# Norm weights on the transposed tokens, one operation for both directions of a recurrence, weight copies on ScalarE, later gates

## The chip, the cores and the metric

The kernel runs on one core of one Trainium2 chip. The metric is the device time of the whole kernel in microseconds (us); a profiled execution also gives a span, from the first to the last instruction. In what follows PE is TensorE (PEld its weight loads), ACT is ScalarE, DVE is VectorE, POOL is GpSimd and SP is SyncE. All times are counted from the start of the span.

## The reference

A first block (attention, a pooling mixer and a mixture of 32 experts, 256 tokens of width 1024) is followed by a second block of two layers. The change touches only the second block:

```
for layer in range(2):
    h = rms_norm_2(x, attn_norm_w[layer])
    a_q, a_i, a_zf, a_zb, a_g, b_u, c_q, c_k, c_v = split(h @ w_in[layer])
    o_a = hgrn2_mixer(a_q, a_i, a_zf, a_zb, a_g, lb_all[layer])
    o_b = fourier_mixer(b_u)
    o_c = dilated_attention_mixer(c_q, c_k, c_v, positions)
    x = x + concatenate([o_a, o_b, o_c]) @ w_out[layer]
    h = rms_norm_2(x, mlp_norm_w[layer])
    x = x + square(relu(h @ w_up[layer])) @ w_down[layer]
return rms_norm_2(x, final_norm_w)
```

`rms_norm_2(x, w)` is x times the reciprocal root of its mean square, times the weight w of each column. `hgrn2_mixer` is a gated recurrence over the 256 tokens in both directions (f = lb + (1 - lb) sigmoid(z), k = 1 - f); `dilated_attention_mixer` rotates queries and keys and takes a softmax over masked scores.

## The kernel before

Every large product is done in three matmuls on a number split in two: the high parts with each other (hi x hi), and each low part with the other's high part. ACT makes the high part of a weight (tile `wh`) by a rounding copy, DVE the low part (`wl`, the weight minus `wh`); both are tiles of 128x1024, four buffers of each, filled from f32 tiles that SP's queue loads. Where a norm weight belongs to the product, `split` gets it as `g` and does each half of a tile by itself: on ACT a copy with a scale per partition, on DVE a scalar_tensor_tensor, 128x512 each (L202 and L203). Without `g` it is one operation of 128x1024 on each engine (L206 and L207). The reciprocal root of a token's norm, `rc`, is made on POOL (L278 to L281 and L1241) from sums of squares made on ACT (L270), and is applied to the product's output.

The tokens stand transposed, as `hT`. `into_hT(t, n)` turns 128 tokens and 512 columns on PE (four transposes into one bank `tp`, L294), copies the high part on ACT (L303) and makes the low part on DVE (L304). There are four such seams of four calls: into mixer 0, MLP 0, mixer 1 and MLP 1.

A mixer does six projections `proj(c0)` of 512 columns: 512 (gates z), 0 (q and v), 1536 (queries), 2048 (keys), 2560 (values cv) and 1024 (g and u), each 48 matmuls of 128x512 into banks `b` (L230 to L232). Between groups of them `bg()` runs one step of each generator that is open:

- `hgrn`, the recurrence. Gates z are transposed (`pz`), then there are eight levels, each with a product `qt` on DVE (L1509), a product `kt` on POOL (L1513; at level 0 a copy on ACT, L1511), small matmuls `hsm` whose results `sl` are masked on DVE (L1490) and summed on POOL, and updates of the running products `hES` (L1545) and `hIP` (L1546) on DVE. Each of the four is done for the forward and the backward direction apart, 128x256 elements each.
- `evac_rot`, the rotation: `rx` and `rt` on DVE, one sum on POOL and one on DVE (L1605 to L1607), then eight transposes `prot` on PE (L1617) and copies on ACT.
- `attention`: scores `sc` (L1643), s on DVE (L1648), maximum, exponentials on ACT, scaling on POOL, transposes `pt`, copies `pT` (L1672; the first of two on DVE, the second on ACT) and products `po` (L1680).

Then follow w_out (`wo`, 96 matmuls) and the MLP, eight times `up` (96 matmuls of 128x256, L240 to L242) and `down` (48 of 128x512, `dn`). Each engine works strictly in the order in which its instructions are queued; a scheduler sets that order when the kernel is built, so a change of the code also moves instructions that it doesn't name.

## Time and profile before

| | us |
|---|---|
| median of 3 runs | 1308.5 (1306.8 to 1309.25) |
| profiled execution | 1306.97 |
| its span | 1305.2 |
| PE busy in the span | 1253.0 (96%) |
| DVE busy | 680.5 (52%) |
| ACT busy | 510.7 (39%) |
| POOL busy | 200.7 (15%) |

The mean granted clock of PE is 0.989 of full speed. The second block begins at about 664 us; mixer 0 lies at 664 to 808, MLP 0 at 808 to 984, mixer 1 at 984 to 1119 and MLP 1 at 1119 to 1296. "Busy" of PE counts matmuls that overlap in its pipeline, so one row of 0.39 us can be followed by the next after 0.23 us: the pitch, from start to start, is what a matmul costs. DVE and ACT overlap by some 0.08 us in the same way.

### The profile page before, as it was taken

The page shows a single profiled execution, that of the slowest core. Times are in us where ns is not written, and L with a number is a line of the kernel's source. Part 1 is how long each engine was busy: PE and PEld are TensorE (multiplying, and loading weights), DVE is VectorE, ACT ScalarE, POOL GpSimd, SP SyncE. Part 2 cuts the span into 40 slices and gives each one's busy share as a digit, 9 for nine tenths or more (in the row PEclk, how much of TensorE's full clock was granted, in tenths as well). Part 3 has the DMA queues.
Part 4 walks back from the last instruction along what each step waited for, and adds up shares of the span by engine and source line. Part 5 has one row for each costly group of instructions (what it writes and reads, how often), then busy time and mean ns, then how long its engine had stood idle before and what let it go on. Part 6 is the DMA issues. An engine that isn't in the chain of part 4 may idle for free. (4 is left out here: it accounts for less than half of the span.)

```text
span 1305.2 us, 19758 instructions
## 1 busy us (share of the span) xinstructions
PE 1253.0 (96%) x7985; PEld 875.2 (67%) x7985; DVE 680.5 (52%) x1164; ACT 510.7 (39%) x919; POOL 200.7 (15%) x270
## 2 busy tenths in 40 slices
PE   6999988999999999899999999999999999999997
PEld 3889976344443443333357678998988767989896
DVE  3698797122122221212157965655557994765654
ACT  2456433111110111101056465555556555655544
POOL 0011030000000000000024541211113461211211
PEclk9999998999999999999999999999999999999999
DMA  9998797999999999999975342655554423555550
GB/s 326 372 340 276 266 381 266 409 416 429 426 429 427 426 427 427 426 428 421 419 305 187 114 130 90 223 181 186 193 193 158 161 82 126 188 177 193 193 162 33
DMA packets 102597, 359.37 MB, mean 275 GB/s; under 512 B 8772, under 2 KB 17856, under 8 KB 87656
## 3 DMA queue, kind: packets, MB, share of 16 engines
q1 hardware_dynamic: 101832, 357.00, 72.1%
q8 instruction: 63, 1.03, 0.3%
q0 software_dynamic: 480, 1.07, 0.2%
q14 instruction: 30, 0.25, 0.1%
q10 hardware_dynamic: 192, 0.02, 0.0%
HBM read 357.00 MB, written 1.06 MB: 274 GB/s over the span
## 5 line engine op out<-in xcount | busy, mean ns | idle before, releaser
L207 DVE TENSOR_TENSOR wl<-w,wh 128x1024 fp32r<-128x1024 f32 x128 | 156.5, 1227 | 100.9 <-ACT wh L206 100.9
L206 ACT CAST wh<-w 128x1024 fp32r<-128x1024 f32 x128 | 134.1, 1050 | 144.4 <-PE up L241 65.8
L202 ACT ACTIVATE wh<-w,vcols 128x512 fp32r<-128x512 f32 x176 | 121.2, 718 | 78.9 <-PE dn L231 34.7
L203 DVE SCALAR_TENSOR_TENSOR wl<-w,vcols,wh 128x512 fp32r<-128x512 f32 x176 | 131.1, 778 | 36.5 <-ACT wh L202 34.4
L241 PE MATMUL up<-hT,wh 128*128 128x256 f32 x512 | 142.4, 278 | 0.0
L242 PE MATMUL up<-hT,wl 128*128 128x256 f32 x512 | 142.4, 279 | 0.0
L240 PE MATMUL up<-hT,wh 128*128 128x256 f32 x512 | 142.4, 278 | 0.0
L1015 PE MATMUL pu<-w,xT 128*64 128x512 f32 x512 | 121.5, 608 | 5.4 <-DMA w<-in_w_expert_up_dram 5.4
L1015 PE MATMUL pg<-w,xT 128*64 128x512 f32 x512 | 119.5, 604 | 0.0
L1101 ACT CAST yh<-y 128x512 fp32r<-128x512 f32 x32 | 19.8, 618 | 253.6 <-DVE y L1100 187.9
L1015 PE MATMUL py<-w,actT 128*64 128x512 f32 x480 | 108.0, 593 | 1.4 <-DMA w<-in_w_expert_down_dram 1.4
L231 PE MATMUL dn<-wh,actl 128*128 128x512 f32 x256 | 101.3, 396 | 0.0
L230 PE MATMUL dn<-wh,acth 128*128 128x512 f32 x256 | 101.2, 395 | 0.0
L232 PE MATMUL dn<-wl,acth 128*128 128x512 f32 x256 | 101.2, 396 | 0.0
L241 PEld LDWEIGHTS up<-hT,wh 128*128 128x128 f32 x512 | 96.9, 189 | 0.6
L240 PEld LDWEIGHTS up<-hT,wh 128*128 128x128 f32 x512 | 96.2, 188 | 0.6
L242 PEld LDWEIGHTS up<-hT,wl 128*128 128x128 f32 x512 | 96.0, 188 | 0.5 <-DVE wl L203 0.5
L1803 POOL TENSOR_TENSOR relu<-relu 128x256 f32<-128x256 f32 x64 | 53.6, 838 | 265.9 <-ACT relu L1802 265.9
L230 PE MATMUL b<-wh,hT 128*128 128x512 f32 x224 | 92.0, 412 | 2.4 <-ACT wh L202 1.9
L232 PE MATMUL b<-wl,hT 128*128 128x512 f32 x224 | 89.4, 403 | 2.3 <-DVE wl L207 1.5
L1100 DVE SCALAR_TENSOR_TENSOR y<-py,ws,gate 128x512 f32<-128x512 f32 x30 | 22.5, 751 | 128.7 <-PE py L1015 127.2
L1015 PEld LDWEIGHTS pu<-w,xT 128*64 128x64 f32 x512 | 38.0, 139 | 76.9 <-issue 67.1
(411 smaller groups left out, 2273.3 us busy)
## 6 DMA issues: line engine op xcount, KB each, us to landing
w<-in_w_expert_up_dram SPq DMA_DIRECT2D x26, 2048.0 KB, 25.7
w<-in_w_expert_down_dram SPq DMA_DIRECT2D x26, 2048.0 KB, 27.2
w<-in_w_expert_gate_dram SPq DMA_DIRECT2D x24, 2048.0 KB, 25.4
w<-in_w_in_dram SPq DMA_DIRECT2D x40, 1024.0 KB, 6.5
w<-in_w_up_dram SPq DMA_DIRECT2D x32, 1024.0 KB, 5.4
w<-in_w_down_dram SPq DMA_DIRECT2D x32, 1024.0 KB, 5.0
w<-in_w_ada_dram SPq DMA_DIRECT2D x24, 1024.0 KB, 9.8
w<-in_w_expert_gate_dram SPq DMA_DIRECT2D x16, 1024.0 KB, 10.3
```

Source lines behind the costliest of these rows:

```text
L202: self.nc.scalar.activation(hi[:, c], v[:, c], AF.Copy, scale=g[:, i:i + 1])
L203: self.nc.vector.scalar_tensor_tensor(lo[:, c], v[:, c], g[:, i:i + 1], hi[:, c].bitcast(F32), op0=ALU.mult, op1=ALU.subtract)
L206: self.last_hi = self.nc.scalar.copy(hi, v).ins
L207: self.last_lo = self.nc.vector.tensor_tensor(lo, v, hi, op=ALU.subtract).ins
L230: nc.tensor.matmul(ps, hT.tok(0, k, t), wh, start=first, stop=False)
L231: nc.tensor.matmul(ps, hT.tok(1, k, t), wh, start=False, stop=False)
L232: nc.tensor.matmul(ps, hT.tok(0, k, t), wl, start=False, stop=last)
L240: nc.tensor.matmul(o, hi[:, c], hT.mov(0, k), start=first and m % 2 == 0, stop=False, skip_group_check=True)
L241: nc.tensor.matmul(o, hi[:, c], hT.mov(1, k), start=False, stop=False, skip_group_check=True)
L242: nc.tensor.matmul(o, lo[:, c], hT.mov(0, k), start=False, stop=last and m % 2 == 1, skip_group_check=True)
L1015: queue["last"] = f(*args, **kw).ins
L1803: nc.gpsimd.tensor_tensor(r, r, r, op=ALU.mult)
```

## The change

Four things change, all in the second block.

1. `split` has no `g` any more: every weight tile is one operation of 128x1024 on ACT and one on DVE. The norm weight is applied in `into_hT` instead, where it is one number per partition: for each of four blocks of 128 columns a copy with a scale on ACT and a scalar_tensor_tensor on DVE, both 128x128.
2. In the recurrence `qt`, `kt`, `hES` and `hIP` are one operation each for both directions (128x512 elements), by an access pattern `runs_of` that steps from one direction's runs to the other's.
3. All copies `pT` are made by ACT.
4. In layer 0 the gates z are not read out right after their projection but at the third step of the next one, and not before the last `wh` issued until then.

```diff
+def runs_of(src, off, step, b, h, wide=True):
+    return bass.AP(tensor=src.tensor, offset=src.offset + off, ap=[list(src.ap[0]), [step, 2], [2 * h, b], [1 if wide else 0, h]])
...
-    def split(self, v, g=None):
+    def split(self, v):
         hi = self.sp.tile([128, 1024], F32R, name="wh", tag="wh")
         lo = self.sp.tile([128, 1024], F32R, name="wl", tag="wl")
-        if g is not None:
-            for i in range(2):
-                c = slice(512 * i, 512 * i + 512)
-                self.nc.scalar.activation(hi[:, c], v[:, c], AF.Copy, scale=g[:, i:i + 1])
-                self.nc.vector.scalar_tensor_tensor(lo[:, c], v[:, c], g[:, i:i + 1], hi[:, c].bitcast(F32),
-                                                    op0=ALU.mult, op1=ALU.subtract)
-            return hi, lo
         self.last_hi = self.nc.scalar.copy(hi, v).ins
         self.last_lo = self.nc.vector.tensor_tensor(lo, v, hi, op=ALU.subtract).ins
         return hi, lo
...
-    def into_hT(self, t, n):
+    def into_hT(self, g, t, n):
         src = self.transposed(self.x[:, t, n * 512:n * 512 + 512])
-        self.split_into(self.hT.t[0][n][:, t], self.hT.t[1][n][:, t], src)
+        for b in range(4):
+            hi, lo = (self.hT.t[i][n][:, t, b] for i in range(2))
+            c = g[:, 4 * n + b:4 * n + b + 1]
+            self.nc.scalar.activation(hi, src[:, b], AF.Copy, scale=c)
+            self.nc.vector.scalar_tensor_tensor(lo, src[:, b], c, hi.bitcast(F32), op0=ALU.mult, op1=ALU.subtract)
...
-                    def half(x, w, h=h):
-                        return x.rearrange("p n (b w h) -> p (n b) w h", w=2, h=h)[:, :, w]
-                    for d in range(2):
-                        nc.vector.tensor_tensor(half(qt, 1 - d), half(qd, 1 - d), half(IP[:, d], 1 - d), op=ALU.mult)
-                        if lv == 0:
-                            nc.scalar.copy(half(kt, d), half(kk[:, d], d))
-                        else:
-                            nc.gpsimd.tensor_tensor(half(kt, d), half(kk[:, d], d), half(ES[:, d], d), op=ALU.mult)
+                    nb = S // h
+                    def given(x, h=h, nb=nb):
+                        return runs_of(x, 0, (0 if tuple(x.shape[1:]) == (2, S) else 2 * S) + h, nb, h)
+                    def taken(x, h=h, nb=nb):
+                        return runs_of(x, h, (0 if tuple(x.shape[1:]) == (2, S) else 2 * S) - h, nb, h)
+                    nc.vector.tensor_tensor(taken(qt), taken(qd), taken(IP), op=ALU.mult)
+                    if lv == 0:
+                        nc.scalar.copy(given(kt), given(kk))
+                    else:
+                        nc.gpsimd.tensor_tensor(given(kt), given(kk), given(ES), op=ALU.mult)
...
-                        for d in range(2):
-                            edge = (lambda x: x[:, :, h - 1:h]) if d == 0 else (lambda x: x[:, :, 0:1])
-                            full = [128, 2 * S // (2 * h), h]
-                            ip, es = IP[:, d], ES[:, d]
-                            nc.vector.tensor_tensor(half(es, d), half(es, d), edge(half(ip, 1 - d)).to_broadcast(full), op=ALU.mult)
-                            nc.vector.tensor_tensor(half(ip, 1 - d), half(ip, 1 - d), edge(half(ip, d)).to_broadcast(full), op=ALU.mult)
+                        nc.vector.tensor_tensor(given(ES), given(ES), runs_of(IP, 2 * h - 1, 2 * S - 2 * h + 1, nb, h, False), op=ALU.mult)
+                        nc.vector.tensor_tensor(taken(IP), taken(IP), runs_of(IP, h - 1, 2 * S + 1, nb, h, False), op=ALU.mult)
...
-                        (nc.scalar.copy if j else nc.vector.tensor_copy)(pT[:, j], pt)
+                        nc.scalar.copy(pT[:, j], pt)
...
-            bgs, tail = [], []
+            bgs, tail, held = [], [], []
             def bg():
+                if held:
+                    held.append(0)
+                    if len(held) == 4:
+                        with self.tc.issue_after(self.last_hi):
+                            evac_z(512, held[0])
+                        held.clear()
...
-                self.tok_part(ps, hT, win, 0, c0, True, False, bg, g=gw[:, 0:4])
+                self.tok_part(ps, hT, win, 0, c0, True, False, bg)
                 for f in late:
                     f()
-                self.tok_part(ps, hT, win, 4, c0, False, True, bg, g=gw[:, 4:8])
+                self.tok_part(ps, hT, win, 4, c0, False, True, bg)
                 e(c0, ps)
-            proj(512, evac_z, late)
+            proj(512, (lambda c0, ps: held.append(ps)) if not layer else evac_z, late)
...
-                    late.append(partial(self.into_hT, t, n))
+                    late.append(partial(self.into_hT, gw, t, n))
...
-                        todo.append(partial(self.into_hT, t, n))
+                        todo.append(partial(self.into_hT, self.norm_cols("attn_norm_w_2", 1), t, n))
```

How the built program moves is seen at three places. The first is ACT's queue around the gates of layer 0, with `mT,ss<-xnew` the sums of squares and `wh` the weights' high parts. Before:

```order
L202 ACTIVATE wh<-w,g_748 128x512
L270 ACTIVATE mT_4637,ss<-xnew 128x512
L202 ACTIVATE wh<-w,g_748 128x512
L1433 ACT_TABLE_LOAD
L1433 ACTIVATE z<-b,rc 128x512
L270 ACTIVATE mT_4637,ss<-xnew 128x512
L202 ACTIVATE wh<-w,g_748 128x512
L1433 ACTIVATE z<-b,rc 128x512
L202 ACTIVATE wh<-w,g_748 128x512 x10
```

and after:

```order
L205 CAST wh<-w 128x1024
L301 ACTIVATE hT_79<-tp,g_748 128x128
L268 ACTIVATE mT_4637,ss<-xnew 128x512
L205 CAST wh<-w 128x1024
L301 ACTIVATE hT_79<-tp,g_748 128x128
L268 ACTIVATE mT_4637,ss<-xnew 128x512
L205 CAST wh<-w 128x1024 x2
L268 ACTIVATE mT_4637,ss<-xnew 128x512
L1436 ACT_TABLE_LOAD
L1436 ACTIVATE z<-b,rc 128x512 x2
L205 CAST wh<-w 128x1024 x4
```

Both z now stand behind the last sum of squares and behind four whole `wh`; before, a sum of squares and a `wh` stood behind the first z and all later `wh` behind the second.

The second place is DVE's queue ahead of the rotation of the keys (the rows `rx<-b,cosr` and `rt<-b,sinr` at the end). Before:

```order
L203 SCALAR_TENSOR_TENSOR wl<-w,g_748,wh 128x512
L1509 TENSOR_TENSOR qt<-hq,hIP 128x32x8 x2
L203 SCALAR_TENSOR_TENSOR wl<-w,g_748,wh 128x512 x2
L1545 TENSOR_TENSOR hES<-hES,hIP 128x32x8 x2
L1546 TENSOR_TENSOR hIP<-hIP 128x32x8 x2
L203 SCALAR_TENSOR_TENSOR wl<-w,g_748,wh 128x512 x2
L1490 TENSOR_TENSOR sl<-hsm,kmix 128x128
L203 SCALAR_TENSOR_TENSOR wl<-w,g_748,wh 128x512
L1490 TENSOR_TENSOR sl<-hsm,kmix 128x128
L1509 TENSOR_TENSOR qt<-hq,hIP 128x16x16 x2
L203 SCALAR_TENSOR_TENSOR wl<-w,g_748,wh 128x512
L1605 TENSOR_TENSOR rx<-b,cosr 128x512
```

and after:

```order
L1517 TENSOR_TENSOR qt<-hq,hIP 128x2x32x8
L206 TENSOR_TENSOR wl<-w,wh 128x1024
L1549 TENSOR_TENSOR hES<-hES,hIP 128x2x32x8
L206 TENSOR_TENSOR wl<-w,wh 128x1024
L1550 TENSOR_TENSOR hIP<-hIP 128x2x32x8
L1493 TENSOR_TENSOR sl<-hsm,kmix 128x128
L206 TENSOR_TENSOR wl<-w,wh 128x1024
L1493 TENSOR_TENSOR sl<-hsm,kmix 128x128
L1517 TENSOR_TENSOR qt<-hq,hIP 128x2x16x16
L1549 TENSOR_TENSOR hES<-hES,hIP 128x2x16x16
L1609 TENSOR_TENSOR rx<-b,cosr 128x512
```

The seven half `wl` have become three whole ones (the fourth stands just ahead of this piece), the pairs of `qt`, `hES` and `hIP` one row each, and the last `hES`, of which one half stood behind `rx`, now stands ahead of it.

The third place is ACT's queue at the seam from mixer 0 into MLP 0 (`junk,ss` are sums of squares, `hT<-tp` the transposed tokens). Before:

```order
L206 CAST wh<-w 128x1024
L202 ACTIVATE wh<-w,vcols 128x512 x3
L270 ACTIVATE junk,ss<-xnew 128x512 x2
L303 CAST hT_78<-tp 128x512 x2
L202 ACTIVATE wh<-w,vcols 128x512 x4
```

and after:

```order
L205 CAST wh<-w 128x1024 x3
L268 ACTIVATE junk,ss<-xnew 128x512 x2
L301 ACTIVATE hT_78<-tp,vcols 128x128 x4
L205 CAST wh<-w 128x1024
L301 ACTIVATE hT_78<-tp,vcols 128x128 x3
L205 CAST wh<-w 128x1024
L301 ACTIVATE hT_78<-tp,vcols 128x128
```

The two copies of 128x512 have become eight pieces of 128x128, with two whole `wh` between them.

## Rows read from the trace of the kernel before

**Rows 1.** Windows: stretch, busy us (and instructions) of each engine, PE clock, DMA.
```profile
808.00:984.00 176.00, 176.00 (x1151) 158.94 (x1149) 102.54 (x133) 98.05 (x168) 30.87 (x40) 1.00 0.57 189
```

**Rows 2.** List of waits of PE, 664 to 1305: total us, times, longest.
```profile
PE prot L1617 <- POOL rx L1607: 5.8, 2, 2.9
...
PE po L1680 <- DVE pT L1672: 2.0, 2, 1.0
...
PE b L230 <- ACT wh L202: 1.9, 2, 1.7
...
PE b L230 <- ACT hT L303: 0.5, 1, 0.5
```

**Rows 3.** Timeline of PE, POOL and ACT at the gates: start, us, [idle before <-releaser].
```profile
689.49 0.39 PE L231 MATMUL b<-wh,hT 128*128 128x512 f32 x1
...
689.72 0.40 PE L232 MATMUL b<-wl,hT 128*128 128x512 f32 x1
...
692.97 0.19 POOL L1241 TENSOR_TENSOR rc<-rs 128x1 f32<-128x1 f32 x1
...
693.20 0.69 ACT L1433 ACTIVATE z<-b,rc 128x512 f32<-128x512 f32 x1 [2.95 <-POOL rc L1241]
...
694.54 0.50 PE L230 MATMUL b<-wh,hT 128*128 128x512 f32 x1 [1.72 <-ACT wh L202]
...
699.32 0.93 PE L1446 MATMUL pz<-ident,z 128*128 128x128 f32 x7
```

**Rows 4.** Timeline of DVE and PE at the rotation, layer 0.
```profile
717.65 0.68 DVE L1605 TENSOR_TENSOR rx<-b,cosr 128x512 f32<-128x512 f32 x1
...
727.10 0.76 DVE L1545 TENSOR_TENSOR hES<-hES,hIP 128x256 f32<-128x256 f32 x2
...
728.44 1.41 DVE L203 SCALAR_TENSOR_TENSOR wl<-w,g,wh 128x512 fp32r<-128x512 f32 x2
...
732.37 0.40 PE L232 MATMUL b<-wl,hT 128*128 128x512 f32 x1
...
732.99 0.68 DVE L1605 TENSOR_TENSOR rx<-b,cosr 128x512 f32<-128x512 f32 x1
...
735.66 0.44 PE L1617 MATMUL prot<-ident,rx 128*128 128x128 f32 x2 [2.90 <-POOL rx L1607]
...
740.41 0.50 PE L230 MATMUL b<-wh,hT 128*128 128x512 f32 x1
```

**Rows 5.** Groups by form, 664 to 808: busy us, mean ns, then idle.
```profile
L207 DVE TENSOR_TENSOR wl<-w,wh 128x1024 fp32r<-128x1024 f32 x8 | 9.6, 1224 | 2.1 <-ACT wh L206 2.1
...
L1490 DVE TENSOR_TENSOR sl<-hsm,kmix 128x128 f32<-128x128 f32 x10 | 2.7, 284 | 0.6 <-PE hsm L1483 0.6
...
L1703 ACT COPY fw<-f 128x127 f32<-128x127 f32 x2 | 0.5, 264 | 0.2 <-DVE fw L1702 0.2
```

**Rows 6.** Groups by form on DVE between the rotations, 717.8 to 733.
```profile
L203 DVE SCALAR_TENSOR_TENSOR wl<-w,g,wh 128x512 fp32r<-128x512 f32 x8 | 6.7, 855 | 0.0
...
L1509 DVE TENSOR_TENSOR qt<-hq,hIP 128x256 f32<-128x256 f32 x4 | 2.1, 570 | 0.0
...
L1546 DVE TENSOR_TENSOR hIP<-hIP 128x256 f32<-128x256 f32 x4 | 2.1, 548 | 0.0
...
L1545 DVE TENSOR_TENSOR hES<-hES,hIP 128x256 f32<-128x256 f32 x4 | 1.8, 462 | 0.0
```

**Rows 7.** Timeline of ACT and DVE at the copies of attention weights.
```profile
764.26 0.56 ACT L1672 COPY pT<-pt 128x512 f32<-128x512 f32 x1
...
764.73 1.04 ACT L206 CAST wh<-w 128x1024 fp32r<-128x1024 f32 x1
...
766.06 0.68 DVE L1672 COPY pT<-pt 128x512 f32<-128x512 f32 x1
```

**Rows 8.** Timeline of ACT and DVE at the seam into MLP 0.
```profile
803.64 1.05 ACT L303 CAST hT<-tp 128x512 fp32r<-128x512 f32 x2
...
804.82 1.28 DVE L304 TENSOR_TENSOR hT<-tp,hT 128x512 fp32r<-128x512 f32 x2
```

## What I predict

> **What bounds the kernel now.** I read the windows by stage first, then the list of TensorE's (PE's) waits, then the timelines around the longest of them, then durations by form. The windows tell where nothing can be won: in the MLP stage PE is busy all 176.00 us at clock 1.00, with DVE and ACT at 58% and 56% [rows 1]. So the ACT and DVE work that the weights lose there, more than half of it by count, is worth nothing. What counts is PE's waits in the two mixers, and the list gives nearly all of them [rows 2]: 5.8 us in two waits for the rotated keys (prot on rx), 2.0 in two for the attention weights (po on pT), 1.9 in two for weights (b on wh), 0.5 for the transposed tokens (b on hT). A wait costs more than its idle time where the clock falls behind it. I therefore take each loss as elapsed time less the matmuls in it at full pitch, 0.229 us from start to start (689.49 to 689.72, [rows 3]).
>
> - First gates, layer 0: after the matmul of 689.72 the next is due at 689.95; pz starts at 699.32. In these 9.37 us the timeline has 18 matmuls (the seventh is that of 694.54), 18 x 0.229 = 4.1. Loss 5.25 us.
> - Rotated keys: last b at 732.37, b again at 740.41 [rows 4]. From 732.60 that is 7.8 us; the 8 prot, 64 hsm and 8 sc between need 2.5 by the pitches that the timeline has for such matmuls at full clock. Loss 5.3, of which 2.9 idle; the same in layer 1, by the equal second wait of [rows 2].
> - Attention weights: 1.0 per layer.
>
> Together 5.25 + 2 x 5.3 + 2 x 1.0 + 0.5 = 18.4 us. Removing waits can win no more.
>
> **The change part by part.**
>
> *Later gates (layer 0).* PE waits at 694.54 for a wh that ACT makes only behind the second z, and that z waits until POOL ends rc at 693.16 [rows 3]. Rc is itself late, since the last sum of squares stood behind the first z. The order after puts all sums of squares and four whole wh ahead of both z. Without z ahead of it I work rc forward to about 692.1 and the end of z to 692.9. PE meanwhile runs the next projection and needs z only at pz, which without the stall is due at 699.32 - 5.1 = 694.2. Margin 1.3 us, so the loss goes almost wholly: **-5.1**. If the sums of squares come later than that (they share ACT with 16 pieces of hT), 1.3 us is free and beyond it pz waits one for one: bound -4.0.
>
> *Recurrence and weights ahead of the rotated keys.* This is the large term. DVE works without a gap, and its rx for the keys begins at 732.99, though the last matmul of their projection had run by 730.05 (twelve matmuls of the next projection fill PE until 732.60). DVE is 2.9 us behind. Between the two rx groups (717.65 and 732.99, [rows 4]) the order before has 8 half wl and 4 half qt, hIP and hES each; after, 4 whole wl and 2 whole of each other. Two half wl with POOL idle beside them take 1.41 (728.44), two half hES 0.76 (727.10); 0.08 of each lies under what follows. A whole wl lasts 1.22 [rows 5], 1.15 without that 0.08, so 0.18 less than the pair. A whole recurrence operation is not in the trace; I price it by the nearest row, rx at 128x512, 0.68 or 0.60 without the 0.08, so 0.07 less than the pair. That gives 4 x 0.18 + 6 x 0.07 = 1.1 us. But the halves in this stretch are stretched: eight wl take 6.7 us where four pairs of 1.41 make 5.6, twelve of the recurrence 6.0 where six of 0.76 make 4.6 [rows 6]. Upper bound of the relief, if the whole operations escape that: 1.1 + 1.1 + 1.4 = 3.6. Lower bound: 0.7, if POOL delays whole ones a little more than halves. Ahead of the first rx group stand one whole wl less (1.15) and one hES more (0.6), of use only as far as that group's own projection is done. I take 2.0 us in layer 0 and 2.7 in layer 1, out of the 2.9. The idle then falls to 0.9 and 0.2. The idle of 1.0 at po was not followed by slow matmuls, that of 1.72 at 694.54 was; so the 2.4 us that the loss has beyond its idle go too, half of them in layer 0 (1.2) and two thirds in layer 1 (1.6). Layer 0: -3.2. Layer 1: -4.3. Together **-7.5**, bounds -1.5 and -10.
>
> A page of the Trainium skill speaks against this term. "SBUF — State Buffer", section "SBUF: two separate sides", states that a DVE operation with two SBUF inputs and a GpSimd operation that reads SBUF take one port pair in turn, and that the loser blocks for the whole instruction. By that rule POOL's kt delay DVE as much in one piece as in two, and the sum would keep the lower bound. The trace agrees in part: DVE's rows do stretch beside POOL, but to 0.86 on average from 0.71 (half of the pair), not by a whole POOL instruction.
>
> *Attention weights on ACT.* Now ACT copies at 764.26, makes a wh and copies again, while DVE's second copy ends at 766.66 without the overlap; po then starts after 1.0 us of idle [rows 7]. After, ACT has two copies, a wh and two copies behind the fourth group of exponentials: 764.26 + 2 x 0.47 + 0.95 + 2 x 0.47 = 767.1. That alone is +0.45. The scores move too: in the order after, from the first sl behind prot DVE has sl, wl, sl, qt, wl (0.2 + 1.15 + 0.2 + 0.6 + 1.15 = 3.3) and then the scores' s, which lags the resumed b by up to 1.85 us where now it starts with it. With the rx wait gone PE comes to po earlier relative to this chain. So po waits longer, by 0.45 to 1.85; I take **+1.4** per layer. That makes a wait of 2.4, longer than the 1.72 that slow matmuls followed, for which I add 0.5 per layer. Both layers: +3.8.
>
> *Norm weight on the tokens.* Each seam has 16 pieces of 128x128 on each of ACT and DVE in place of 4 operations of 128x512. ACT's nearest row is the 128x127 copy, 0.26 us, DVE's the 128x128 sl, 0.28 [rows 5]. In the built order a hi piece waits for the lo piece before it, and whole wh and wl stand between pieces. At the two seams into the MLPs PE now has the first up matmul directly behind the first tp; before, a wo stood there that no list shows waiting. That up needs two hi pieces, behind both sums of squares and a wh that is 0.3 longer: 0.3 + 0.26 + 0.1 = about +0.65 each. The rest of hT hides behind twenty wo matmuls (4.6 us). The seam into mixer 1 waits 0.5 for hT already [rows 2]; +0.15. The seam into mixer 0 I count at 0: the longer hT and the shorter weights cancel in what ACT and DVE have to do before pz. Sum **+1.4**; without the cover, see the second rival.
>
> Sum: -5.1 - 7.5 + 3.8 + 1.4 = -7.4. The profiled execution took 1306.97 us, so 1299.6; the median of the runs shown is 1.5 above it, hence **1301** against 1308.5.
>
> **Rivals.**
>
> *DVE's relief does not reach rx.* Kt becomes one operation as long as two and holds up a whole wl where it held up a half, so rx comes hardly earlier. Then it is z against po and the seams: -5.1 - 1.5 + 2.3 (po at the mean of its bounds, no slow clock) + 1.4 = -2.9, about 1305.5. For it: the stretching in [rows 6]. Against: the pairs that POOL leaves alone shorten in any case. It is where the skill's rule leads. Chance 0.17.
>
> *Slower: the pieces go back and forth.* In a seam hi and lo alternate between ACT and DVE, with a whole wl between lo pieces: 0.3 + 0.3 + 1.15 a step, three steps after the first piece, 5.2 us, against 2.3 for both tiles now [rows 8]. Where PE has run out of other matmuls by then, each of the four seams costs 2.9: +11.6 in place of the +1.4, so -7.4 + 10.2 = +2.8, about 1311. It decides once a seam costs 2.2 us on average. Against: the 4.6 us of other matmuls behind each first half. Chance 0.07. The skill has the reason for the order of such pieces ("PSUM — Partial Sum Buffer", "PSUM bank collisions raise a hardware error"): no two engines may be in one bank's quadrant at once. No row here shows one.
>
> *More than expected.* Rx starts at its projection's end in both layers, and the scores come early enough with it for po: -5.1 - 9.5 + 0.9 + 0.7 = -13, 1295.5. Chance 0.10.
>
> **How the numbers follow.** The forecast has 0.66, spread over -4 to -11. I call 0.2%, 2.6 us, what can be told from no change. Faster: 0.61 of the forecast, the 0.10, and half of the first rival: 0.79. Slower: 0.07. Same: the rest, 0.14. The range 1296 to 1306.5 takes in the first rival and reaches to the third, and leaves out the slower one.
>
> **What would show it.** Right: both z behind one another with no wait for wh between 690 and 695, and clock 1.00 there; prot idle under 1 us, and rx of the keys within 1 us of its projection's end; po idle over 2 us; the first up waiting 0.6 for hT. Wrong: prot still idle near 2.9, with whole hES or hIP at twice a half's duration or more; waits for hT of 2 us at the seams; slow matmuls behind po or prot.

## The result, and the profile after

The changed kernel is slower. Its median over seven runs is 1317.39 us (1315.93 to 1324.35) against 1309.25 us for seven runs of the kernel before on the same chip; the ratio is 1.008, with an interval of 1.0061 to 1.0100. The profiled execution took 1321.54 us (span 1319.8). DVE's busy time fell from 680.5 to 665.5 us and ACT's from 510.7 to 491.7, and the kernel became longer all the same. The two profiled executions lie on either side of their medians (1306.97 against 1309.25, 1321.54 against 1317.39), so they differ by 14.6 us where the medians differ by 8.1: what follows takes that one pair of executions apart.

Ahead of the second block's first transposes (`tp`), where nothing was changed, executions differ by several us (tp comes between 668.5 and 675.6). So I compare intervals from tp to the end: 633.8 us in the profile of before, 646.6 in that of after, 12.8 more. The table comes from the starts of PE's rows: before in us, every other column the difference to it. "prot" is the first transpose of rotated queries, then of rotated keys; "sc" the first scores, then the second group; "MLP 0" runs from the first `tp` of that seam to the first of the next.

```
interval      before  after     e1     e2     e3     e4     e5     e6     e7     e8
tp to pz        27.9  -4.08  -0.25  -4.11  -0.27  -5.13  -4.11  -5.13  -4.08  -2.28
pz to prot      23.3  +1.13  +0.00  +0.96  +0.09  +1.28  +0.96  +1.38  +0.93  +1.09
prot to prot    13.1  +2.32  +1.30  +1.23  +0.04  +1.92  +1.23  +3.31  +0.97  +2.33
prot to sc       3.0  +0.96  +1.38  +0.30  +0.12  +0.23  +0.29  +1.38  +0.23  +0.97
sc to sc         4.8  +1.59  -0.22  +0.25  +1.30  +0.22  +0.55  +0.22  +0.84  -0.17
sc to po        21.8  +1.53  +0.03  +0.44  -0.02  +0.00  +1.47  +0.00  +0.96  +2.00
po to wo        14.1  -0.67  -0.33  +0.46  +0.46  +0.01  +1.28  +1.01  +1.30  -0.66
MLP 0          180.4  +3.06  +0.00  +3.05  +0.06  +0.03  +2.24  +0.03  +2.24  +0.50
tp to pz, 1     21.1  +1.16  +0.01  +1.16  +0.01  -0.01  +1.18  -0.01  +1.18  +0.59
prot to prot    13.1  +1.01  +1.29  -0.36  -0.01  +0.01  -0.34  +1.29  -0.19  +1.00
prot to sc       2.7  +1.03  +1.34  +0.39  -0.44  -0.23  +0.58  +1.41  +0.41  +1.24
sc to sc         5.0  +0.73  +0.41  +0.96  +0.63  +1.81  +0.52  +0.01  +0.93  -0.64
sc to po        21.8  +1.53  -0.01  +0.36  -0.01  +0.03  +1.48  +0.03  +0.97  +3.75
po to wo        14.1  -0.68  -0.33  +0.45  +0.45  -0.60  +2.60  +0.99  +1.27  -0.67
tp to end      192.3  +2.25  +0.02  +2.17  -0.04  +0.06  +3.10  -0.02  +3.05  +0.50
all            633.8 +12.84  +4.64  +7.71  +2.36  -0.39 +12.97  +5.84 +10.95  +9.48
```

The gates were won (-4.1). Everything else that was to be won or to cost little went the wrong way: the keys +4.9 and +2.8 (three rows from prot to the second sc), the seams +3.1, +1.2 and +2.3, the attention +0.9 in each layer (sc to po less what po to wo gives back).

The list of PE's waits after (664 to 1322; total us, times, longest), to be held against [rows 2]:

```profile
PE prot L1621 <- POOL rx L1611: 8.0, 2, 4.1
PE pt L1675 <- DVE s L1652: 2.6, 2, 1.3
PE up L240 <- DVE wl L206: 2.3, 2, 1.1
...
PE up L238 <- ACT hT L301: 1.8, 2, 0.9
PE b L230 <- DVE wl L206: 1.2, 3, 0.5
PE prot L1621 <- DVE rx L1611: 0.8, 1, 0.8
PE b L228 <- ACT hT L301: 0.6, 1, 0.6
```

The waits for wh (1.9) and for pT (2.0) are gone. The wait for the rotated keys, which was to shrink, grew from 5.8 to 8.0, and three waits are new: pt, and two in the first `up`.

At the gates, the timeline of PE, POOL and ACT after, against [rows 3]:

```profile
690.60 0.19 POOL L1243 TENSOR_TENSOR rc<-rs 128x1 f32<-128x1 f32 x1
691.29 0.69 ACT L1436 ACTIVATE z<-b,rc 128x512 f32<-128x512 f32 x1
694.59 0.50 PE L230 MATMUL b<-wl,hT 128*128 128x512 f32 x1 [0.18 <-DVE wl L206]
...
696.25 0.69 ACT L1436 ACTIVATE z<-b,rc 128x512 f32<-128x512 f32 x1 [4.28 <-POOL rc L1243]
...
697.00 1.03 PE L1449 MATMUL pz<-ident,z 128*128 128x128 f32 x8
```

No wait for wh is left and the granted clock is 1.00 from 690 to 700. The second z now ends 0.06 us before pz: it waits for its own rc, so the margin of 1.3 is used up, near the bound of -4.0.

At the rotated keys of layer 0, the timeline of DVE, POOL and PE, against [rows 4]:

```profile
731.34 0.75 DVE L1517 TENSOR_TENSOR qt<-hq,hIP 128x512 f32<-128x512 f32 x1
731.50 1.73 POOL L1521 TENSOR_TENSOR kt<-hk,hES 128x512 f32<-128x512 f32 x1
...
732.29 0.40 PE L230 MATMUL b<-wl,hT 128*128 128x512 f32 x1
733.27 0.93 DVE L1549 TENSOR_TENSOR hES<-hES,hIP 128x512 f32<-128x512 f32 x1 [1.18 <-POOL kt L1521]
734.12 0.68 DVE L1609 TENSOR_TENSOR rx<-b,cosr 128x512 f32<-128x512 f32 x1
...
736.79 0.69 PE L1621 MATMUL prot<-ident,rx 128*128 128x128 f32 x2 [4.11 <-POOL rx L1611]
...
743.31 0.63 PE L230 MATMUL b<-wl,hT 128*128 128x512 f32 x1
743.74 0.63 PE L228 MATMUL b<-wh,hT 128*128 128x512 f32 x1
```

`hES` is updated in place, and `kt` reads the old `hES`. In one piece, the update stands still until POOL has finished the whole kt, and rx stands behind it in DVE's queue. DVE, which had no gap here before, idles 1.18 us ahead of this hES, and 3.5 in three such waits up to here. PE waits 4.11 instead of 2.90, and the matmuls that follow run for a while at a pitch of 0.43 (743.31 to 743.74).

The longer wait is not all rx's doing. Counted from tp, rx starts at 60.95 us, where before it started at 61.58: it is 0.6 earlier. PE is through with its matmuls at 59.51 in place of 61.35, 1.8 earlier, because the wait at the gates is gone. With the recurrence as before and the rest of the change (e5 below) rx starts at 59.65 in layer 0, and at 61.11 in place of 62.47 in layer 1 (from that layer's tp). So the joined recurrence delays rx by 1.3 and 1.4 us; the rest of the longer wait in layer 0 is the gates' gain, met again as a wait.

Groups by form, DVE and POOL, 664 to 820 (busy, mean ns, then idle ahead of them):

```profile
L206 DVE TENSOR_TENSOR wl<-w,wh 128x1024 fp32r<-128x1024 f32 x36 | 45.6, 1275 | 13.7 <-ACT wh L205 13.7
L1517 DVE TENSOR_TENSOR qt<-hq,hIP 128x512 f32<-128x512 f32 x8 | 7.0, 872 | 0.0
L1549 DVE TENSOR_TENSOR hES<-hES,hIP 128x512 f32<-128x512 f32 x7 | 6.2, 879 | 5.8 <-POOL kt L1521 5.8
L1550 DVE TENSOR_TENSOR hIP<-hIP 128x512 f32<-128x512 f32 x7 | 6.1, 878 | 0.1
...
L302 DVE SCALAR_TENSOR_TENSOR hT<-tp,vcols,hT 128x128 fp32r<-128x128 f32 x12 | 3.8, 344 | 2.2 <-ACT hT L301 2.2
...
L1521 POOL TENSOR_TENSOR kt<-hk,hES 128x512 f32<-128x512 f32 x7 | 12.0, 1714 | 2.4 <-PE hsm L1486 2.4
```

Mixer 0 as a whole, `tp` to `tp`, in a window of after (columns as in [rows 1]):

```profile
673.17:807.17 134.00, 126.77 (x1081) 97.24 (x1082) 90.07 (x133) 76.33 (x148) 55.50 (x68) 0.96 0.44 149
```

The same window of before, 671.41 to 802.66, has DVE busy 98.12 of 131.25. So the change does take 8 us off DVE here, and the mixer lasts 2.75 longer. Qt, hES and hIP take 19.3 us where the halves took 20.9 (7.1, 7.6 and 6.2 in the same stretch of before), so 1.6 us of busy time is saved and 5.8 us of waiting added.

The mean of 0.87 is not the price of a whole operation. With POOL at rest it takes 0.68, rx's time, as predicted (0.69 with almost none beside it, at 759.26 below). The long ones, up to 1.83, overlap a POOL operation that began before them, as in this timeline of DVE and POOL after:

```profile
740.32 1.65 DVE L1517 TENSOR_TENSOR qt<-hq,hIP 128x512 f32<-128x512 f32 x1
...
740.16 1.27 POOL L1521 TENSOR_TENSOR kt<-hk,hES 128x512 f32<-128x512 f32 x1 [0.24 <-PE hsm L1486]
```

Kt ends at 741.43 and qt 0.55 us later. So do all of them: of the products qt, the updates hES and hIP and the wl that last over 0.08 us longer than alone in the second block, 38 before and 26 after, each ends 0.28 (128x256), 0.55 (128x512) or 1.08 us (128x1024) after a POOL operation that began first.

In the attention of layer 0 the same wait stands ahead of the scores; the timeline of DVE, PE and ACT, against [rows 7]:

```profile
759.26 0.69 DVE L1549 TENSOR_TENSOR hES<-hES,hIP 128x512 f32<-128x512 f32 x1 [2.31 <-POOL kt L1521]
...
761.73 0.68 DVE L1652 SCALAR_TENSOR_TENSOR s<-sc,kmix 128x512 f32<-128x512 f32 x1
...
762.47 0.66 PE L1675 MATMUL pt<-ident,s 128*128 128x128 f32 x4 [1.32 <-DVE s L1652]
...
767.59 1.04 ACT L1676 COPY pT<-pt 128x512 f32<-128x512 f32 x2
...
769.48 1.06 ACT L1676 COPY pT<-pt 128x512 f32<-128x512 f32 x2
...
770.35 1.95 PE L1684 MATMUL po<-pT,cv 128*64 128x256 f32 x16
```

The two pairs of copies with a `wh` between are as foreseen, but po does not wait for them: pt waits earlier, for s.

At the seam into MLP 0, the timeline of ACT, DVE and PE, against [rows 8]:

```profile
808.47 0.60 ACT L301 ACTIVATE hT<-tp,vcols 128x128 fp32r<-128x128 f32 x2
808.85 0.35 DVE L302 SCALAR_TENSOR_TENSOR hT<-tp,vcols,hT 128x128 fp32r<-128x128 f32 x1 [0.57 <-ACT hT L301]
809.12 1.22 DVE L206 TENSOR_TENSOR wl<-w,wh 128x1024 fp32r<-128x1024 f32 x1
809.13 0.38 PE L238 MATMUL up<-hT,wh 128*128 128x256 f32 x1 [0.92 <-ACT hT L301]
809.24 0.37 ACT L301 ACTIVATE hT<-tp,vcols 128x128 fp32r<-128x128 f32 x1 [0.16 <-DVE hT L302]
810.63 0.37 ACT L301 ACTIVATE hT<-tp,vcols 128x128 fp32r<-128x128 f32 x1 [1.03 <-DVE hT L302]
...
815.28 0.35 DVE L302 SCALAR_TENSOR_TENSOR hT<-tp,vcols,hT 128x128 fp32r<-128x128 f32 x1 [0.31 <-ACT hT L301]
...
816.82 0.38 PE L240 MATMUL up<-hT,wl 128*128 128x256 f32 x1 [1.14 <-DVE wl L206]
```

A hi piece waits for the lo piece of the other engine, and that lo stands behind a whole wl (810.63). The first hi starts at 808.47, the last of the eight lo (815.28) ends 7.2 us later. Both the first up (0.92) and later its wl (1.14) come late. These two waits make 2.1 of the seam's 3.06, and of the 2.25 at the seam into MLP 1; where the other 1.0 comes from is not shown. Behind the seam PE is full again, as in [rows 1] (window, columns as there): 174.70 of 176 us at clock 1.00.

```profile
814.00:990.00 176.00, 174.70 (x1138) 157.89 (x1137) 99.95 (x108) 88.82 (x140) 37.45 (x39) 1.00 0.57 188
```

### The profile page after: what moved, and what is told of

The parts are those of the page before. It is cut to its first block, busy times and chain, and to the rows that moved or that the text cites. A ratio compares the mean times of both kernels' runs of the same rounds, so it can differ in the third digit from the quotient of the medians.

```text
span 1319.8 us, 19578 instructions
## 1 busy us (share of the span) xinstructions
PE 1259.5 (95%) x7985; PEld 878.0 (67%) x7985; DVE 665.5 (50%) x1048; ACT 491.7 (37%) x861; POOL 211.7 (16%) x256
## 5 line engine op out<-in xcount | busy, mean ns | idle before, releaser
L206 DVE TENSOR_TENSOR wl<-w,wh 128x1024 fp32r<-128x1024 f32 x240 | 296.2, 1237 | 172.8 <-ACT wh L205 172.8
L205 ACT CAST wh<-w 128x1024 fp32r<-128x1024 f32 x240 | 251.1, 1050 | 276.8 <-PE dn L229 71.3
L1812 POOL TENSOR_TENSOR relu<-relu 128x256 f32<-128x256 f32 x64 | 60.7, 949 | 253.8 <-ACT relu L1811 253.8
L228 PE MATMUL b<-wh,hT 128*128 128x512 f32 x224 | 92.7, 416 | 0.6 <-ACT hT L301 0.6
L229 PE MATMUL b<-wh,hT 128*128 128x512 f32 x224 | 90.0, 403 | 0.1
L276 POOL TENSOR_SCALAR ms<-ss 128x1 f32<-128x1 f32 x12 | 3.9, 323 | 506.6 <-DVE yl L1104 458.4
```

The costliest lines, as they stand in the source:

```text
L205: self.last_hi = self.nc.scalar.copy(hi, v).ins
L206: self.last_lo = self.nc.vector.tensor_tensor(lo, v, hi, op=ALU.subtract).ins
L228: nc.tensor.matmul(ps, hT.tok(0, k, t), wh, start=first, stop=False)
L229: nc.tensor.matmul(ps, hT.tok(1, k, t), wh, start=False, stop=False)
L1812: nc.gpsimd.tensor_tensor(r, r, r, op=ALU.mult)
```

## The experiments

Each median stands beside that of the kernel before on the same chip, over five rounds, with the ratio and its interval. In what was expected, theory A says that the joined hES waits for the joined kt and holds up rx, and theory B that the alternation of hi and lo makes the seams long; other theories say there what they hold.

**e1 to e4: each of the four parts alone.** e1 has of the change only

```diff
+                    nc.vector.tensor_tensor(taken(qt), taken(qd), taken(IP), op=ALU.mult)
...
+                        nc.gpsimd.tensor_tensor(given(kt), given(kk), given(ES), op=ALU.mult)
...
+                        nc.vector.tensor_tensor(given(ES), given(ES), runs_of(IP, 2 * h - 1, 2 * S - 2 * h + 1, nb, h, False), op=ALU.mult)
```

> The kernel before with only the recurrence's operations joined (qt, kt, hES, hIP one each for both directions). Theory A (a whole hES must wait for the whole kt that reads it on POOL, so DVE stands still ahead of the rotation): waits of DVE for kt of 4 to 6 us per layer as in the changed kernel, prot idle about 4 us in place of 2.9 in both layers, slow matmuls behind it, the time 4 to 6 us longer than before (about 1314). Rival D (the whole wl of 128x1024, not the recurrence, make DVE late): prot idle 2.9 or less, time the same or up to 2 us shorter.

1312.36 against 1307.91, 1.0040 (1.0027 to 1.0053). The prot wait, and in DVE's timeline the hES ahead of rx:

```profile
PE prot L1624 <- POOL rx L1614: 8.3, 2, 4.2
```

```profile
733.84 0.93 DVE L1552 TENSOR_TENSOR hES<-hES,hIP 128x512 f32<-128x512 f32 x1 [1.18 <-POOL kt L1524]
```

A part made to relieve DVE costs 4.6 us of the interval by itself. Counted from tp, rx starts 1.0 us later than before in layer 0 and 1.3 in layer 1. Theory A holds for the place and the time; the waits for kt are 1.2 us per layer, fewer than the 4 to 6 expected.

e2 has only the norm weight on the tokens:

```diff
+        for b in range(4):
...
+            self.nc.scalar.activation(hi, src[:, b], AF.Copy, scale=c)
+            self.nc.vector.scalar_tensor_tensor(lo, src[:, b], c, hi.bitcast(F32), op0=ALU.mult, op1=ALU.subtract)
```

> The kernel before with only the norm weights moved to the transposed tokens. Theory B (hi and lo pieces go back and forth between ACT and DVE): first up of each MLP waits about 0.9 us for hT and the first wl behind the second half about 1.1, the seam into mixer 1 about 1.3 in all, together 5 to 6 us longer at the seams; mixers 0 to 2 us shorter, prot idle 2 to 2.9; time 3 to 6 us longer (about 1313). Rival D: prot idle 4 here as well, time 8 us longer or more.

1316.48 against 1307.91, 1.0067 (1.0051 to 1.0084). All three seams of after are there (+3.05, +1.16, +2.17). The wait of the gates is gone too, -4.11, though z stands in its old place in the code. The time and a prot wait of 4.0 in layer 0 are what rival D expected, but its reason is not there: from tp, rx starts 1.9 us earlier than before (59.66 against 61.58), and PE is there 3.0 earlier. In layer 1, with nothing won at the gates, prot waits 2.5. Whole weights alone shorten prot to prot in layer 1 by a mere 0.36. Between the two rx groups of layer 1 DVE takes 15.1 us where it took 15.3: four whole wl save 1.5 (5.1 against 6.7 for eight halves), but one more hES (0.6) stands ahead of rx, and a pair of qt lasts 1.82 in place of 0.75, because each half now meets a kt.

e3 has only the copies:

```diff
-                        (nc.scalar.copy if j else nc.vector.tensor_copy)(pT[:, j], pt)
+                        nc.scalar.copy(pT[:, j], pt)
```

> The kernel before with only the copies pT moved to ACT. Prediction's term: po waits about 1.45 in place of 1.0, +0.5 per layer, time +1 (1310). Rival C (the new wait of pt in the changed kernel, 1.3 us per layer, comes from ACT's copies): pt waits over 1 us and the time is 3 us longer or more. Theory A says that pt does not wait here.

1310.34 against 1307.91, 1.0023 (1.0008 to 1.0039). Po to wo is 0.46 longer in each layer, the 0.45 of the prediction; pt waits for nothing, so the pt wait of after is not the copies' doing. The rest of its 2.4 in the interval lies in sc to sc, in the stretch of matmuls at a lower clock behind the unchanged prot wait. The ratio makes 3 us of time, more than the 1 that was expected.

e4 has only the later gates (`last_hi` also taken from the scaled halves):

```diff
+                    if len(held) == 4:
+                        with self.tc.issue_after(self.last_hi):
+                            evac_z(512, held[0])
```

> The kernel before with only the later gates of layer 0 (issued behind the last scaled half wh made until then). Theory: pz 4 to 5 us earlier, and all of mixer 0 with it, time 4 to 5 us shorter (about 1304.5), prot idle still 2.9. Rival E (the gain is given back, because DVE's work and not pz sets when the rotated queries and keys come): prot idle of layer 0 over 5 us, time within 2 us of before.

1307.66 against 1307.91, 0.9993 (0.9981 to 1.0006): nothing, though tp to pz shrinks by 5.13 where 5.1 was predicted. By the second sc 3.65 of it is given back, and prot waits 4.3 in layer 0, with the recurrence as before:

```profile
PE prot L1617 <- POOL rx L1607: 7.2, 2, 4.3
```

Rival E has the time right, and the wait short of its 5 us. In the timeline on DVE one sees why:

```profile
696.26 4.06 DVE L203 SCALAR_TENSOR_TENSOR wl<-w,g,wh 128x512 fp32r<-128x512 f32 x6 [2.69 <-ACT wh L202]
700.24 1.28 DVE L1462 COPY hIP<-pz 128x512 f32<-128x512 f32 x2
```

PE has pz at 695.38, but DVE takes it up at 700.24, behind six half wl: 27.6 us after tp, where before it was 28.5. DVE gained 0.9 of PE's 5.1. The 1.5 us that this one profile keeps up to the second sc are not in the medians; layer 1 of it has 1.0 more than before, where the edit changes nothing.

**e5 and e6: the change without one part.** e5 takes back part 2, e6 part 1:

```diff
-                    nc.vector.tensor_tensor(taken(qt), taken(qd), taken(IP), op=ALU.mult)
...
+                    for d in range(2):
+                        nc.vector.tensor_tensor(half(qt, 1 - d), half(qd, 1 - d), half(IP[:, d], 1 - d), op=ALU.mult)
```

> The changed kernel with the recurrence as before, direction by direction. Theory A: DVE no longer waits for kt, prot idle 2 us or less in both layers, no slow matmuls behind the scores; 6 to 9 us shorter than the changed kernel (about 1310). Rival D (whole wl make rx late): prot idle stays at 3.5 to 4, within 2 us of the changed kernel.

1319.79 against 1309.21, 1.0080 (1.0057 to 1.0103): no better than after. Its list of PE's waits has

```profile
PE prot L1613 <- POOL rx L1603: 6.6, 2, 4.0
PE po L1676 <- ACT pT L1668: 3.6, 4, 1.0
```

DVE no longer waits for kt, and rx starts 1.3 and 1.4 us earlier than after. In layer 1 the prot wait falls from 3.9 to 2.6. In layer 0 it is 4.0 still, as in e2 and e4, because PE is there early. The keys (three rows from prot to the second sc) stand at +2.1 and +0.8, where after has +4.9 and +2.8. But po now waits 1.0 and 0.8 us in each layer for ACT's copies pT, and po to wo is +1.28 and +2.60 where after has -0.7; in layer 1 the granted clock in that stretch is 0.90 (1079.83 to 1096.49). So theory A is right about DVE's wait, and wrong about PE's wait in layer 0 and about the time. Rival D has the time and layer 0's wait right, for another reason than it gives.

```diff
-            self.nc.scalar.activation(hi, src[:, b], AF.Copy, scale=c)
-            self.nc.vector.scalar_tensor_tensor(lo, src[:, b], c, hi.bitcast(F32), op0=ALU.mult, op1=ALU.subtract)
+        self.split_into(self.hT.t[0][n][:, t], self.hT.t[1][n][:, t], src)
```

> The changed kernel with the norm weights in the weights again. Theory B: waits for hT and for the first wl at the three seams gone, 4.5 to 6 us shorter than the changed kernel (about 1312); prot idle still about 4 by theory A, 3 or less by rival D.

1313.21 against 1309.21, 1.0035 (1.0021 to 1.0050), 7.0 us less than after in the interval; the seams are as before. Of the two parts taken back, this is the one that shortens the changed kernel. Prot is at its worst, 9.3 in two (5.1 in layer 0, where PE is early).

**e7 and e8: the two suspects mended inside the changed kernel.** e7 does kt and hES by direction again, qt and hIP joined:

```diff
-                        nc.gpsimd.tensor_tensor(given(kt), given(kk), given(ES), op=ALU.mult)
+                        for d in range(2):
+                            nc.gpsimd.tensor_tensor(given(kt)[:, d], given(kk)[:, d], given(ES)[:, d], op=ALU.mult)
...
+                        for d in range(2):
+                            nc.vector.tensor_tensor(given(ES)[:, d], given(ES)[:, d], edge[:, d], op=ALU.mult)
```

> The changed kernel with kt and hES direction by direction again, qt and hIP whole. Theory A (the wait is that of a whole hES for a whole kt): DVE's waits for kt fall from about 5.8 us in layer 0 to under 1, rx of the keys comes 1.2 us earlier or more, prot idle under 3 us, 3 to 7 us shorter than the changed kernel. Rival F (POOL and DVE only slow each other, and longer operations more so): POOL's work is the same, so rx and prot idle stay within 0.5 us of the changed kernel.

1319.63 against 1309.21, 1.0069 (1.0044 to 1.0095). The list of DVE's waits, 695 to 745, has

```profile
DVE hES L1552 <- POOL kt L1522: 1.9, 3, 0.6
```

against 3.5 in three (1.2 the longest) of after: half the operation, half the wait. From tp, rx starts 1.6 and 1.2 us earlier than after, so rival F is out. Prot to prot falls by 1.35 and 1.20, and pt's wait from 2.6 to 1.3 us in two. But po waits 1.6 for pT, so that 1.9 us of interval is all that is left, too little for the medians. Theory A expected less waiting for kt than that, prot under 3 us (it is 3.9 in layer 0, 2.7 in layer 1) and 3 to 7 us of time.

e8 does a tile's four hi pieces, then its four lo:

```diff
         for b in range(4):
...
+            self.nc.scalar.activation(his[b], src[:, b], AF.Copy, scale=cols[b])
+        for b in range(4):
+            self.nc.vector.scalar_tensor_tensor(los[b], src[:, b], cols[b], his[b].bitcast(F32), op0=ALU.mult, op1=ALU.subtract)
```

> The changed kernel with the pieces of a transposed tile issued as four high parts and then four low parts. Theory B (the alternation delays the seam): ACT no longer waits for DVE's lo pieces, the wait of 1.1 us for the first wl at each MLP's second half goes, 2 to 4 us shorter than the changed kernel. Rival G (the pieces' number and ACT's sums of squares ahead of them, not the alternation, set the seam): first up still waits 0.9 us or more, time within 1.5 us of the changed kernel.

1316.91 against 1309.21, 1.0051 (1.0034 to 1.0069). The three seams fall from 3.06, 1.16 and 2.25 to 0.50, 0.59 and 0.50. The same seam in its timeline, ACT and DVE:

```profile
808.23 2.15 ACT L301 ACTIVATE hT<-tp,vcols 128x128 fp32r<-128x128 f32 x8
...
809.38 2.16 DVE L303 SCALAR_TENSOR_TENSOR hT<-tp,vcols,hT 128x128 fp32r<-128x128 f32 x8 [0.21 <-ACT hT L301]
```

From the first hi to the end of the last lo it is 3.3 us, in after 7.2. Theory B holds. At the first seam the new order loses 1.8 (b waits 1.7 for the lo part).

**e9 to e14: does it help to bring the keys out of DVE's way, in the kernel before?** The table of these runs:

```
interval      before     e9    e10    e11    e12    e13    e14    e15    e16    e17
tp to pz        27.9  -0.26  -4.18  +0.12  -0.23  -0.25  -4.70  -2.30  -2.27  -0.12
pz to prot      23.3  +0.00  +1.29  +0.01  -0.01  -0.01  +1.28  +0.98  +0.93  +0.09
prot to prot    13.1  +0.63  +1.94  +0.21  -1.75  -3.06  -2.51  -2.99  -3.05  -3.03
prot to sc       3.0  -0.82  -0.24  +0.12  -0.80  -1.13  -1.14  -1.31  -1.31  -1.14
sc to sc         4.8  -0.95  -0.95  +1.08  -0.72  -0.71  -0.72  -0.72  -0.73  -0.72
sc to po        21.8  +3.39  +3.39  +0.01  +0.72  +5.09  +6.61  +6.29  +2.33  +6.69
po to wo        14.1  +0.76  +0.85  -0.58  +0.53  +0.96  -0.52  -1.12  +1.29  -0.66
MLP 0          180.4  +0.04  +0.05  +0.03  +0.07  +0.03  +0.03  +0.50  +1.31  +0.04
tp to pz, 1     21.1  +0.00  +0.00  +0.00  +0.01  +0.00  -0.01  +0.61  +0.59  +0.00
prot to prot    13.1  +0.60  +0.59  +0.18  -1.76  -3.08  -3.08  -3.08  -3.08  -3.07
prot to sc       2.7  -0.58  -0.53  +0.52  -0.52  -0.85  -0.85  -1.03  -1.03  -0.86
sc to sc         5.0  -1.18  -1.18  +0.53  -0.97  -0.95  -0.97  -0.96  -0.97  -0.97
sc to po        21.8  +3.41  +3.37  +0.01  +0.69  +5.10  +6.59  +6.27  +2.28  +3.84
po to wo        14.1  +1.06  +1.07  -0.43  +0.57  +0.94  -0.50  -1.08  +1.27  +0.48
tp to end      192.3  -0.02  -0.01  -0.06  +0.03  -0.04  +0.07  +0.53  +1.35  +0.02
all            633.8  +6.07  +5.49  +1.75  -4.16  +2.07  -0.40  +0.59  -1.06  +0.54
```

e9 turns the keys and begins the attention one step later; e10 adds part 4 to it (the diff of e4).

```diff
             def attention():
+                yield
...
-            proj(2048, evac_rot(kT, bgs, 0))
+            proj(2048, evac_rot(kT, bgs, 1))
```

> The kernel before with the transposes of the rotated keys, and the attention behind them, one step (12 matmuls of the next projection, 2.75 us) later in PE's order. Theory H (PE waits for rx only because DVE is 2.9 us late, and the slow matmuls behind it are the price of that idle time): prot idle under 0.5 us and no slow matmuls in both layers, pt or po wait up to 2 us more later on; 4 to 9 us shorter than before (about 1302). Rival I (attention's chain from scores to po is what ends last, so that PE waits there instead): pt and po wait 3 us or more per layer in addition, time within 2 us of before.

> The same with the later gates of layer 0. Theory J (the gates' 5 us are lost again because PE meets DVE's unchanged lateness at prot): with 2.75 us more of cover, part of them stays, 2 to 4 us shorter than the keys alone (about 1299). Rival E (DVE paces the whole of mixer 0): within 1.5 us of the keys alone.

e9: 1315.29 against 1309.79, 1.0038 (1.0022 to 1.0054). e10: 1314.33, 1.0031 (1.0013 to 1.0048). The long prot wait is gone and 1.1 to 1.2 us is won up to the second sc. Behind it pt waits 4.1 and po 4.6 (2.0 before): +4.2 and +4.5, as rival I says and more. The later gates help no more here than alone (rival E).

e11 joins qt and hIP, which no kt reads or writes, and leaves kt and hES by direction (lines as in e7):

> The kernel before with only qt and hIP joined, kt and hES by direction. Theory A (the wait of a whole hES for a whole kt is what the joined recurrence costs): prot idle 3 us or less, no longer than before by more than 1 us (1307 to 1309.5), 3 to 5 us shorter than all four joined. Rival F (joined operations are slowed beside POOL): prot idle near 4, about 1312.

1309.17 against 1309.79, 0.9997 (0.9985 to 1.0010). The prot wait is near that of before:

```profile
PE prot L1627 <- POOL rx L1617: 6.1, 2, 3.1
```

Joining as such does no harm and brings nothing; e1 less e11 is the price of joining kt and hES, 0.43% by the ratios.

e12 leaves out the updates of hES and hIP at levels 2 and 3, so that part of the recurrence is not computed:

```diff
-                    if lv < 7:
+                    if lv < 7 and lv not in (2, 3):
```

> The kernel before with the updates of hES and hIP left out at levels 2 and 3 of the recurrence (16 operations of 128x256 in all, the result changes): some 2.7 us less work for DVE ahead of the rotated keys in each layer. Theory H (DVE's lateness alone sets the wait): prot idle under 1 us in both layers, slow matmuls gone, 6 to 11 us shorter than before (about 1300). Rival K (rx is late because of what comes before DVE, weights or the projection): prot idle still over 2 us, under 3 us shorter.

1302.60 against 1309.79, 0.9948 (0.9933 to 0.9963). With less to do on DVE the prot wait falls from 2.9 to 1.1 at its longest, and most of what is won stays won (2.0 us or more in each mixer), as theory H expected, though with a prot wait under 1. So less work on DVE does shorten the mixer.

e13 queues the later wl and the updates behind the keys' rx; e14 adds part 4:

```diff
+                with self.tc.issue_after(late) if late else ExitStack():
+                    self.nc.vector.scalar_tensor_tensor(lo[:, c], v[:, c], g[:, i:i + 1], hi[:, c].bitcast(F32),
...
+                            with tc.issue_after(self.behind[0]) if getattr(self, "behind", None) else ExitStack():
...
+                    if not steps:
+                        self.behind = turned, 1
```

> The kernel before with no work changed, but DVE's later low parts and the later updates of hES and hIP queued behind the rotation of the keys (only the first wl of the next projection may go ahead). Theory L (it is what stands ahead of rx in DVE's queue, not its total, that makes PE wait): rx of the keys within 1 us of its projection's end, prot idle under 0.7 us, no slow matmuls behind it, 5 to 10 us shorter than before in all (about 1302). Rival I (attention's or the recurrence's chain ends last, as with the keys turned later): diag, cross, pt or po wait what prot waited less, time within 2 us of before.

> The same with the later gates of layer 0. If only prot swallowed the gates' gain, 3 to 5 us shorter than the last one. Rival M (the copies hIP still stand behind eight half wl on DVE, so that the recurrence and rx start no earlier): within 1.5 us of the last one.

e13: 1309.65 against 1308.55, 1.0003 (0.9983 to 1.0022). e14: 1308.06, 0.9992 (0.9972 to 1.0012). The rx wait is gone wholly, with no slow matmuls behind it: -4.9 in each layer up to the second sc. It is all given back, +6.0 up to wo. The list of PE's waits in e13 is headed by

```profile
PE b L236 <- DVE wl L207: 9.4, 5, 2.9
```

so PE waits for the weights that were put behind rx. Theory L is right about rx and prot and wrong about the time. From the first hIP copy to pt, DVE of the kernel before is busy 55.33 of 56.89 us: what is put ahead in its queue is taken from what stands behind.

**e15 to e17: the good pieces together.** e15 is e13 with part 1 in the order of e8; e16 adds part 3 and the joining of e11; e17 is e16 with the weights scaled as before.

```diff
+            self.nc.scalar.activation(his[b], src[:, b], AF.Copy, scale=cols[b])
...
+                            for d in range(2):
+                                nc.vector.tensor_tensor(given(ES)[:, d], given(ES)[:, d], edge[:, d], op=ALU.mult)
...
+                        nc.scalar.copy(pT[:, j], pt)
```

> Rx ahead of the rest as in the kernel before last, with the norm weights on the transposed tokens in the order of four high and four low parts. By the seams measured so far +1.5 to +2 us there, by pz 2 to 4 us earlier, and by whole wl some DVE time less: within 3 us of the kernel with rx ahead alone. If the norm weights on the tokens are worth something once rx no longer waits, it is 2 us shorter or more.

> The changed kernel mended by what the runs showed: norm weights on the tokens with four high and then four low parts, qt and hIP joined but kt and hES by direction, copies on ACT, rx of the keys ahead of the rest, gates as before. Theory N (DVE's total between the gates and the attention weights sets the mixer's end): DVE has some 2.4 us of copies and about 1 us of joined operations less per layer than with rx ahead and the norm weights on the tokens; 2 to 3 us per layer shorter than that (about 1304), waits of b for wl smaller. Rival O (ACT, POOL or a chain of latencies ends last there): within 2 us of before.

> The same with the norm weights in the weights as before, so without the cost at the seams. Theory N: DVE loses 2.4 us of copies and about 1 us of joined operations per layer against the kernel with rx ahead alone; 3 to 6 us shorter than before (about 1304). Rival O: within 2 us of before, with waits at pt or po in place of those for wl.

e15: 1309.16 against 1308.55, 0.9995 (0.9977 to 1.0014). e16: 1304.80 against 1308.67, 0.9972 (0.9955 to 0.9990). e17: 1305.14, 0.9971 (0.9955 to 0.9986). E16 and e17 are 0.3% shorter than the kernel before, near the times of theory N; after is 0.8% longer than before. In e16 sc to po costs 2.3 where e13 pays 5.1, and the wait for wl has shrunk:

```profile
PE b L234 <- DVE wl L210: 4.1, 7, 1.0
PE po L1694 <- ACT pT L1686: 2.2, 4, 0.8
```

The window of mixer 0, `tp` to `tp`, in e16:

```profile
671.77:800.22 128.45, 123.10 (x1081) 94.68 (x1082) 88.79 (x140) 75.98 (x148) 61.35 (x75) 1.00 0.46 158
```

With nearly the same DVE work as after (88.79 to 90.07 us) it lasts 5.6 us less. DVE's waits for kt are 2.3 us there, 5.8 in after, and the granted clock is 1.00 in place of 0.96; since the order of the queue differs too, how much each of these brings is not shown.

## Why the prediction was wrong, by its steps

**Later gates, -5.1.** The size was right (-5.13 alone, -4.08 in after). Two things were not. Part 1 removes the same wait by itself (e2: -4.11; the seam into mixer 0, which I counted at 0), so part 4 adds nothing to it. And the gain was counted as if it reached the end; e4 gives 3.65 of it back by the second sc and its median keeps none, because the recurrence goes on DVE's time and not on PE's. To price a wait of PE I should have asked which engine the next wait of PE is for, and whether that one too is earlier.

**Recurrence and weights, -7.5: the step that failed.** The keys measure +4.9 and +2.8. Not all of that is this term: with the recurrence as before (e5) +2.1 and +0.8 stay, in layer 0 mostly the gates' gain given back, as e4 gives back 2.4 in the same rows. The joined recurrence itself costs 2.8 and 2.0 there, and 2.5 and 3.0 alone (e1), where relief was forecast. The sentence "I price it by the nearest row, rx" is not the fault: a whole operation does take 0.68 with POOL at rest. The fault is a wait that the term puts at nothing: hES overwrites what kt reads. In halves, one direction's update could go on while POOL was at the other direction's kt; whole, DVE waits for all of it, 5.8 us in mixer 0 of after. The order after even showed the last hES ahead of rx, and I charged 0.6 for it. The relief by whole weights was too high as well: where they come alone, prot in layer 1 waits 2.5 in place of 2.9 (e2), where the term as a whole forecast 0.2. The first rival had the right place, "kt becomes one operation as long as two", but let it end at no gain instead of a loss.

I weighed that rival by a rule of the Trainium skill ("SBUF — State Buffer", section "SBUF: two separate sides"): of a DVE operation with two SBUF inputs and a POOL operation that reads SBUF, the one that starts first keeps the port pair for its whole length and the other stands still. I wrote that the trace agrees in part. That was a mean of held and free operations; row by row the trace agrees in full: each held DVE operation ends a fixed time after POOL's (0.55 us at 128x512), whole wl take 1.21 to 1.23 when free, and rx and rt, which read a PSUM bank, keep their 0.67 to 0.68 beside POOL. That joining wins nothing from POOL's kt shows too: between pz and the rotated keys of layer 0 it holds DVE up by 3.2 us in before and 3.4 in e1, by an estimate (what the held rows last beyond the free ones). The 1.18 at 733.27 is another thing, a wait that ends with kt.

**Attention weights, +3.8.** About +0.9 per layer in after, in place of 1.9. The copies' own 0.45 was right (e3: 0.46). The rest was put at po; after has it at pt, behind a hES that waits 2.31 for kt (759.26). When that wait is halved (e7) or absent (e5), po does wait for pT, 1.6 and 3.6 in all.

**Norm weight on the tokens, +1.4.** The largest error beside the recurrence: +6.5 over three seams (3.06 + 1.16 + 2.25), 2.2 each. The second rival had the mechanism, the alternation with a whole wl between the pieces. Its point of decision was 2.2 a seam over four seams; measured are 2.2 over three, and a gain at the fourth, into mixer 0. I gave it 0.07, because other matmuls were to cover it. They cover the second half of hT, but not the up that stands directly behind the first tp. E8 shows that the order of the pieces makes 4.9 of the 6.5 (2.6, 0.6 and 1.7). Their duration was mis-sized too: 0.344 for a lo, 0.36 to 0.37 for a hi, in place of 0.28 and 0.26. The Trainium skill forbids two engines one bank's quadrant at the same time ("PSUM — Partial Sum Buffer", section "PSUM bank collisions raise a hardware error"). The trace agrees, in that the program keeps the two apart: in e8 the first lo starts 0.21 us of idle after DVE was free, when the first tile's four hi pieces, and not only its own, are done.

**The sum.** With what each term measured in after: tp to pz -4.1, given back +1.1 at once; keys +7.6; attention +1.7; seams +6.5; together +12.8. That is the pair of profiled executions; the medians differ by 8.1. The sign turned because the two terms that measure largest had the wrong sign or a fifth of their size. Of the parts, taking back the norm weight on the tokens shortens the changed kernel (e6) and so does mending its order (e8); taking back the joined recurrence does not (e5, e7), though alone it costs 0.4% (e1).

**What stays open.** E17's timed gain (0.29%) is clear, yet its profile shows +0.5: the profile is one execution. How long the slow matmuls last behind a prot wait differs between executions (sc to sc -0.2 in e1, +1.3 in e3, with prot waits of 4.2 and 2.9), and I found no rule for it. That e5 loses through pT all that it wins at prot is read from one profile; e5 with the copies on DVE was not run.

## What to carry to other kernels

Before two operations are joined into one, look for what another engine reads or writes of the same tile: halves let two engines work past each other, and a whole must wait for a whole. When two executions are compared, count times from a common event, here tp, and ask of a longer wait whether its end came later or its start earlier. Ask which engine's queue paces a stage before you count another engine's waits in it: a new order of that queue only moves the wait, and less work on it helps only if the engine isn't made to wait instead. When a bank's evacuation is split into pieces for two engines, let the first engine do all of its pieces before the second starts, and look at what waits for the second engine's: at the first seam of e8 that order lost 1.8 us.

## What the runs showed of the hardware

- A qt, a wl or an update of hES or hIP on DVE that meets a POOL operation begun before it ends a fixed time after that one: 0.28 us for 128x256, 0.55 for 128x512 and 1.08 for 128x1024, in all 64 rows of before and after that it lengthens by more than 0.08 us. Qt beside kt thus lasts 1.65 at 740.32, in place of 0.68. The rows of rx, rt and s, which read a PSUM bank, last 0.66 to 0.69 with or without POOL beside them.
- POOL's joined kt has twice the elements and takes 1714 ns on average against 961 for a half, so joining saves POOL 1.3 us in a mixer (13.3 to 12.0). The shortest are 1.27 us and 0.72.
- After an idle of 4.11 us PE's matmuls came at a pitch of 0.43 (743.31 to 745.87), and at 0.23 again from 746.25. The granted clock is 0.50 from 736.8 to 746.2, the lower of the two levels, 1.2 and 2.4 GHz, and 1.00 from 746.3 on. In e13 the same stretch has no long idle, and the granted clock from 728 to 760 is 1.00 where before it is 0.95.
